# Six edits to a hand-ordered Trainium2 kernel: the order's port model, small GpSimd instructions, the sample tile last, and the first two weight loads

## The chip, the cores and the metric

The kernel runs on one NeuronCore of one Trainium2 chip. The metric is the device time of one execution in microseconds (us), the median of several runs. The engines are TensorE (PE in the profile, its weight loads PEld), VectorE (DVE), ScalarE (ACT), GpSimd (POOL) and SyncE (SP), which issues all DMAs of the kernel before.

## What is computed

One inference step of a one-layer encoder with three groups of heads, for a prompt of 512 tokens (four tiles of 128) and a sample of 32 tokens that has caches. Cut to what matters:

```
z = rmsnorm(x, g) @ w_in                   # 1024 -> 3880 columns, split below
A: qa, ka, va, ga   6 heads x 64           # chunk-band attention with a position bias
B: qb, kb, vb, gb   6 heads x 64, rotary   # attention to the best 128 (sample: 256) keys per query
   qi, ki, wi       8 x 32, 32, 8          # the indexer that scores the keys for B
M: qm, gm           4 heads x 64           # attention to 256 memory tokens, keys mk, mv from w_mem_kv
x = x + concat(oA*silu(ga), oB*silu(gb), oM*silu(gm)) @ w_out
y = rmsnorm(x, g_final)
```

Outputs are y for prompt and sample, and the new keys and values. All is float32. Where a product has to be exact enough, an operand is split into a part rounded to the fast float32r form (names that end in h) and the rest (names that end in l), and three products are added: h·h, l·h and h·l.

## The kernel before

**The order is made at build time.** `Line` (line 47) keeps a clock for each engine and a time at which each region of a tile will be ready. Every instruction is issued through `Timed` (253), which advances these clocks by a cost (`cost`, 67). Work is written as generators that yield the time at which they want to go on; a heap runs the earliest. So the position of an instruction in its engine's queue follows from modelled times, while on the chip each queue runs in order and waits on semaphores for what it needs. `port` (166) models that VectorE and GpSimd can't both use the SBUF port that they share: an instruction that would start while the other engine holds the port is moved to the end of that stretch. `least` and `scaled` choose between engines by these clocks. `warm` (727) puts matmuls of an identity matrix into TensorE's queue where the model sees a wait before the first real group is done.

**The head.** `x_load` (630) loads the transposed x in four pieces of two 128-row blocks, the first piece in two DMAs; three buffers, so the fourth waits for the first piece to be used up. `w_load` (473) loads weight pieces in the order of `w_list`; the first four are the indexer's (2 blocks x 296 columns = 592). `START` (36) is the order of the loads on SP's queue: w a weight piece, x a piece of x, t the rotary tables, r natural rows for the norms, m memory rows. `x_split` (651) makes xTh on ScalarE (an activation with scale g) and xTl on VectorE, block by block; `w_split` (488) makes wh on ScalarE and wl on VectorE for pieces 0 and 2 (`WV`), on GpSimd for all others. `index_group` (816) is the first real work of TensorE: four chunks (c = 0 to 3), each with a weight piece and two blocks of x, each for the token tiles 1, 2, 3, 0 with three products per block. It needs xTh, xTl, wh and wl of its chunk. After it come the sample's rows (`w_sample`) and the projections of `EARLY` and `LATE` (43, 44), attention, and the output projection.

**Norms and small instructions.** `norms` (686): ScalarE squares and sums a tile, GpSimd adds EPS, raises to -0.5 (rs) and divides by 16 (r16). `i_done` (799) copies and scales the indexer's head weights wI with rs, then r16, on GpSimd. `load_tables` (763) scales the rotary tables by rs on GpSimd, in eight instructions of 128x64. The load of the memory gain gT[1] is issued after all of `START` (751).

**The tail.** `out_part` (1639) makes the output projection. The last loop (1716) goes over two halves of 512 columns, and in each over the tiles in the order NT, 0, 1, 2, 3, where NT is the sample (32 rows, computed as 64 rows of two halves). A prompt tile takes 18 matmuls of 256 columns, the sample tile 12. For the last tile (`apart`) the 512 columns are evicted in two pieces of 256. `residual` (1670) adds x on VectorE, for the sample in two instructions; `settle` (1689) sums squares on ScalarE, adds up the pieces' sums (VectorE for all but the last piece, with a pointer operand), adds and takes the power on GpSimd, scales one half of the row on VectorE and the other on ScalarE (on VectorE for tile NT - 2), and stores the row.

## Time and profile before

| | us |
|---|---|
| median of 3 runs | 363.46 (363.11 to 363.86) |
| the profiled execution, its own time | 362.68 |
| its span, first to last instruction | 360.6 |
| TensorE busy within the span | 350.7 (97%) |
| VectorE / ScalarE / GpSimd busy | 276.6 / 219.6 / 191.0 |
| granted TensorE clock, mean | 0.996 |

The span is what the trace shows; the profiled execution took 2.1 us more than its span. Times in the trace count from the span's start. Matmul ends are modelled, so a matmul's duration is longer than the step to the next one; where steps matter, starts are compared. A row of the timeline gives start, duration, engine, line, operation, output and inputs, form and count, and in brackets the idle time of the engine before it and what ended that. Nearly all instructions carry the line of `Timed` (L273), so groups are told apart by tiles.

### The profile page before, as it was taken

How to read it: one execution, taken by the hardware profiler on the slowest of the kernel's cores; microseconds unless marked ns; L12 is line 12 of the kernel's file. 1: busy time of each engine (PE TensorE's matmuls, PEld its weight loads, DVE VectorE, ACT ScalarE, POOL GpSimd, SP SyncE). 2: the span in 40 equal slices, each digit the busy share in tenths (PEclk: the TensorE clock that was granted, in tenths of full speed). 3: DMA queues.
4: the chain of work that ended last, by engine and by line, in shares of the span. 5: the costliest groups of instructions: out<-in, count | busy, mean ns of one | idle time of the engine just before them, and what ended most of it. 6: DMA issues, size and time to landing. Idle time of an engine off the chain costs nothing.

```text
span 360.6 us, 7941 instructions
## 1 busy us (share of the span) xinstructions
PE 350.7 (97%) x2961; PEld 320.0 (89%) x2961; DVE 276.6 (77%) x696; ACT 219.6 (61%) x521; POOL 191.0 (53%) x213
## 2 busy tenths in 40 slices
PE   8999999999999999999999999999999999999991
PEld 8989988999998989898699898999979878888991
DVE  3665977797888978888999885999868576866463
ACT  5856767896747775595856553217665665544443
POOL 1778983375465574148436464534597412140751
PEclk9999999999999999999999999999999999999998
DMA  7998351475493322531203250133489412000015
GB/s 251 362 362 264 97 176 58 126 202 147 119 293 119 88 52 62 182 90 44 90 3 87 88 166 20 51 108 115 128 294 362 133 45 104 2 2 2 0 40 209
DMA packets 41478, 46.35 MB, mean 129 GB/s; under 512 B 5184, under 2 KB 36544, under 8 KB 41440
## 3 DMA queue, kind: packets, MB, share of 16 engines
q1 hardware_dynamic: 41440, 45.85, 39.9%
q8 instruction: 23, 0.38, 0.4%
q14 instruction: 15, 0.12, 0.1%
HBM read 39.67 MB, written 6.16 MB: 127 GB/s over the span
## 4 chain that ended last, share of the span: by engine, by line
PE 89%; DVE 4%; DMA 2%; issue 1%; ACT 1%; POOL 1%; SPq 1%; POOLq 0%; ACTq 0%; DVEq 0%
PE bank L273 89%; DMA raw<-in_w_in_dram 2%; POOL ss L273 1%; DVE ysel L273 1%; ACT sq L273 1%; DVE xr L273 1%; SPq L273 1%; DVE z L273 1%; DVE m L273 0%; DVE xTl L273 0%; DVE gate L273 0%; ACT wh L273 0%; ACT xTh L273 0%; DVE o L273 0%; DVE pt L273 0%
## 5 line engine op out<-in xcount | busy, mean ns | idle before, releaser
L273 POOL TENSOR_TENSOR wl<-raw,wh 128x512 fp32r<-128x512 f32 (+2 forms) x68 | 110.0, 1622 | 78.2 <-ACT wh L273 74.4
L273 ACT ACTIVATE wh<-raw 128x512 fp32r<-128x512 f32 (+2 forms) x70 | 50.1, 719 | 33.1 <-issue 13.6
L273 PE MATMUL bank<-wh,xTh 128*128 128x384 f32 (+1 forms) x192 | 65.3, 340 | 0.0
L273 PE MATMUL bank<-wl,xTh 128*128 128x384 f32 (+1 forms) x192 | 63.3, 330 | 0.0
L273 PE MATMUL bank<-wh,xTl 128*128 128x384 f32 (+1 forms) x192 | 63.2, 329 | 0.1
L273 ACT ACTIVATE z<-z,st 128x256 f32<-128x256 f32 (+3 forms) x77 | 41.0, 550 | 21.0 <-DVE st L273 20.9
L273 PE MATMUL bank<-xTh,wh 128*128 128x272 f32 x208 | 46.3, 304 | 0.0
L273 PE MATMUL bank<-xTh,wl 128*128 128x272 f32 x208 | 43.0, 288 | 0.0
L273 PE MATMUL bank<-xTl,wh 128*128 128x272 f32 x208 | 43.0, 288 | 0.0
L273 PEld LDWEIGHTS bank<-wh,xTh 128*128 128x128 f32 x192 | 36.1, 188 | 2.3 <-issue 1.6
L273 PEld LDWEIGHTS bank<-wh,xTl 128*128 128x128 f32 x192 | 36.2, 189 | 0.4 <-DVE xTl L273 0.3
L273 PEld LDWEIGHTS bank<-wl,xTh 128*128 128x128 f32 x192 | 36.1, 188 | 0.2 <-POOL wl L273 0.2
L273 PEld LDWEIGHTS bank<-xTh,wh 128*128 128x128 f32 x208 | 32.7, 189 | 1.7 <-issue 0.8
L273 PEld LDWEIGHTS bank<-xTh,wl 128*128 128x128 f32 x208 | 32.6, 189 | 0.1
L273 PEld LDWEIGHTS bank<-xTl,wh 128*128 128x128 f32 x208 | 32.6, 188 | 0.0
L273 DVE MAX8 m<-ysel 128x8 f32<-128x256 f32 (+2 forms) x48 | 26.4, 549 | 0.0
L273 DVE MATCH_REPLACE8 ysel<-m,ysel 128x256 f32<-128x256 f32 (+2 forms) x48 | 26.1, 543 | 0.0
L273 PE MATMUL bank<-ident,z 128*128 128x128 f32 (+1 forms) x161 | 25.0, 273 | 0.0
L273 ACT COPY pt<-bank 128x512 f32<-128x512 f32 (+1 forms) x26 | 14.1, 543 | 14.3 <-PE bank L273 14.2
L273 DVE SCALAR_TENSOR_TENSOR ysel<-r,wI,ysel 128x256 f32<-128x256 f32 (+2 forms) x21 | 17.8, 849 | 6.0 <-ACT r L273 5.6
L273 POOL TENSOR_TENSOR oBl<-o,oBh 128x128 fp32r<-128x128 f32 (+1 forms) x9 | 4.9, 549 | 30.4 <-ACT oBh L273 30.4
L273 PEld LDWEIGHTS bank<-ident,z 128*128 128x128 f32 (+1 forms) x161 | 18.2, 140 | 2.5 <-issue 1.0
(307 smaller groups left out, 892.6 us busy)
## 6 DMA issues: line engine op xcount, KB each, us to landing
raw<-in_w_in_dram SPq DMA_DIRECT2D x20, 384.0 KB, 3.6
raw<-in_w_in_dram SPq DMA_DIRECT2D x26, 256.0 KB, 2.9
raw<-in_w_out_dram SPq DMA_DIRECT2D x8, 384.0 KB, 3.1
nat<-in_x_prompt_dram SPq DMA_DIRECT2D x4, 512.0 KB, 7.9
raw<-in_w_mem_kv_dram SPq DMA_DIRECT2D x8, 256.0 KB, 2.8
xr<-in_x_prompt_dram SPq DMA_DIRECT2D x4, 512.0 KB, 4.8
out_dram<-xr SPq DMA_DIRECT2D x4, 512.0 KB, 2.6
xr<-in_x_t_dram SPq DMA_DIRECT2D x3, 544.0 KB, 5.8
```

The source lines that it names most:

```text
L273: return fn(*args, **kw)
```

## The change

Six things are changed.

- **Port model.** In `port`, a VectorE instruction is pushed behind GpSimd's stretch once and then stops; a GpSimd instruction is pushed only in a narrower case for VectorE (`kept`), and a VectorE instruction that takes the port pushes GpSimd's clock by its own length. GpSimd's memsets and one-column instructions get costs of their own.
- **First loads.** gT[0] and the weight pieces 0 and 1 are issued on ScalarE's queue, ahead of all else; SP's queue begins with x. `START` loses the two w's and is put in another order.
- **Weight piece 0.** Both wh and wl are made on VectorE, block by block, and chunk 0 of `index_group` runs block by block: all four tiles with xTh·wh, then xTh·wl, then xTl·wh.
- **Small instructions.** EPS is added on VectorE; r16 goes, the 1/16 sits in ScalarE's copy of wI, and wI is scaled by rs twice in one GpSimd instruction. The rotary tables' scaling waits until two units of attention are scored. In `settle`, the running sum of a later piece goes from VectorE to GpSimd.
- **gT[1]** is loaded with the first tables.
- **The tail.** The sample tile comes last in both halves and is the one that is evicted in two pieces; the row half on VectorE is that of tile 3, not 2.

```diff
-START = "wxwxwxwtwwwwrrrrrmmrr"
+START = "xxwwxtwwwwrrrrrmmrr"
...
+        if op == "memset":
+            return 0.05 + n / 1000.0
+        if n == 1:
+            return 0.57 if kw.get("op") == ALU.pow else 0.22
         return 0.15 + n * (0.0034 if op == "tensor_scalar" else 0.0021)
...
         for s, end, by in self.taken:
-            if by != eng and s <= t < end:
+            if by != eng and s <= t < end and (eng == "POOL" or t > self.kept + 0.02):
                 t = end
+                if eng == "DVE":
+                    break
+        if eng == "DVE":
+            if self.clk["POOL"] > t:
+                self.clk["POOL"] += d
+            self.kept = t + d
...
+    DMA2 = Timed(line, "ACTQ", nc.scalar)
...
-            DMA.dma_start(raw, w[k * P:(k + nk) * P, lo:hi].rearrange("(k p) n -> p k n", p=P))
+            (DMA2 if i < 2 else DMA).dma_start(raw, w[k * P:(k + nk) * P, lo:hi].rearrange("(k p) n -> p k n", p=P))
...
+            if i == 0:
+
+                wh = pw.tile(list(raw.shape), F32R, tag="wh", name="wh", bufs=n)
+                wl = pw.tile(list(raw.shape), F32R, tag="wl", name="wl", bufs=n)
+                for k in range(2):
+                    yield line.at(raw) - 0.2
+                    V.tensor_copy(wh[:, k], raw[:, k])
+                    tsub(V, wl[:, k], raw[:, k], f(wh)[:, k])
+                split.append((wh, wl))
+                continue
...
-            G.tensor_scalar(ss[:n, i:i + 1], ss[:n, i:i + 1], EPS, None, op0=ALU.add)
+            V.tensor_scalar(ss[:n, i:i + 1], ss[:n, i:i + 1], EPS, None, op0=ALU.add)
             G.tensor_tensor(rs[:n, i:i + 1], ss[:n, i:i + 1], nhalf[:n], op=ALU.pow)
-            G.tensor_scalar(r16[:n, i:i + 1], rs[:n, i:i + 1], 1.0 / 16, None, op0=ALU.mult)
...
-    DMA.dma_start(gT[0], a["norm_mix_g"])
+    DMA2.dma_start(gT[0], a["norm_mix_g"])
     line.until(lambda g=x_load(): next(g, 1) == 1)
+    allowed[0] = 2
+    line.spawn(w_load())
+    line.until(lambda: len(raws) == 2)
...
         def scale():
+            yield from line.wait(lambda: count["scored"] > 1)
...
-            A.copy(wI[:, t, :], acc[:, 288:296])
+            A.activation(wI[:, t, :], acc[:, 288:296], AF.Copy, scale=1.0 / 16)
...
-            for r in (rs, r16):
-                G.tensor_scalar(wI[:, t, :], wI[:, t, :], r[:, t:t + 1], None, op0=ALU.mult)
+            r = rs[:, t:t + 1]
+            G.tensor_scalar(wI[:, t, :], wI[:, t, :], r, r, op0=ALU.mult, op1=ALU.mult)
...
+            for kk in range(2) if c == 0 else ():
+                for xs, ws in ((xTh, w[0]), (xTh, w[1]), (xTl, w[0])):
+                    for t in (1, 2, 3, 0):
+                        c0, c1 = (256, 288) if t == 0 else (0, 296)
+                        x = xs[0][:, kk, t * P:(t + 1) * P]
+                        yield x, ws[:, kk, c0:c1]
+                        PE.matmul(acc[t][:, c0:c1], x, ws[:, kk, c0:c1], start=(kk == 0 and xs is xTh and ws is w[0]), stop=False)
...
-            V.tensor_scalar(run, new, EPS if j == 0 else old, None, op0=ALU.add)
+            if j == 0:
+                V.tensor_scalar(run, new, EPS, None, op0=ALU.add)
+            else:
+                G.tensor_tensor(run, new, old, op=ALU.add)
...
-        if t == NT - 2:
+        if t == NT - 1:
...
-                          (NT, 0, 1, 2, 3), (NT - 1,) if c0 else ()))
+                          (0, 1, 2, 3, NT), (NT,) if c0 else ()))
```

## Rows read from the trace of the kernel before

**Rows 1.** The page: its first line, and busy time, share of the span and instructions of each engine.

```profile
span 360.6 us, 7941 instructions
PE 350.7 (97%) x2961; PEld 320.0 (89%) x2961; DVE 276.6 (77%) x696; ACT 219.6 (61%) x521; POOL 191.0 (53%) x213
```

**Rows 2.** Busy time by stretch (us from the span's start): length, then busy time and instructions of PE, PEld, DVE, ACT and POOL, granted clock, DMA share, GB/s. Two answers are put together here; the first two rows hold nothing but fillers on PE.

```profile
1.36:4.00 2.64, 2.64 (x12) 2.64 (x13) 0.00 (x0) 1.03 (x3) 0.28 (x2) 1.00 0.64 186
...
6.00:7.18 1.18, 1.18 (x12) 1.18 (x12) 0.99 (x2) 0.54 (x1) 0.00 (x0) 1.00 0.98 329
...
7.18:20.48 13.30, 13.25 (x101) 12.81 (x99) 8.98 (x11) 8.89 (x13) 9.31 (x8) 1.00 1.07 370
20.48:352.70 332.22, 331.47 (x2832) 301.36 (x2831) 263.02 (x678) 205.05 (x498) 178.57 (x192) 1.00 0.37 115
352.70:360.60 7.90, 0.15 (x2) 0.00 (x0) 2.46 (x6) 2.01 (x7) 1.49 (x4) 0.81 0.49 199
150.00:200.00 50.00, 49.62 (x435) 43.72 (x432) 45.72 (x130) 35.22 (x91) 26.95 (x25) 1.00 0.19 57
```

**Rows 3.** Who PE's weight load waited for over the whole span: us in total, times, longest.

```profile
PEld bank L273 <- DVE st L273: 1.3, 3, 0.7
...
PEld bank L273 <- ACT mTh L273: 0.4, 1, 0.4
```

**Rows 4.** The timeline of the first microseconds, PE: the fillers, and the first matmul of chunks 0, 1, 2 and 3 of the index group, with the one in chunk 1 that waited.

```profile
1.36 6.06 PE L273 MATMUL bank<-ident 128*128 128x128 f32 x32 [1.36 <-POOL nhalf L273]
7.18 0.38 PE L273 MATMUL bank<-wh,xTh 128*128 128x296 f32 x1
...
10.54 0.39 PE L273 MATMUL bank<-wh,xTh 128*128 128x296 f32 x1
...
11.58 0.40 PE L273 MATMUL bank<-wh,xTl 128*128 128x296 f32 x1
...
14.17 0.38 PE L273 MATMUL bank<-wh,xTh 128*128 128x296 f32 x1
...
17.28 0.38 PE L273 MATMUL bank<-wh,xTh 128*128 128x296 f32 x1
```

**Rows 5.** The timeline of SP's queue from 0: the first issues.

```profile
0.73 0.39 SPq L273 DMA_DIRECT2D g_mix<-in_norm_mix_g_dram  x1
1.18 0.89 SPq L273 DMA_DIRECT2D xr<-in_x_t_dram  x2
```

**Rows 6.** The timeline of ACT from 0; the wait for a DMA in brackets tells when it landed.

```profile
0.73 1.28 ACT L273 ACT_TABLE_LOAD   x1 [0.73 <-PEq L1768]
...
5.84 0.70 ACT L273 ACTIVATE wh<-raw 128x592 fp32r<-128x592 f32 x1 [0.28 <-DMA raw<-in_w_in_dram]
7.72 0.75 ACT L273 ACTIVATE xTh<-xr,g_mix 128x544 fp32r<-128x544 f32 x1 [1.19 <-DMA xr<-in_x_t_dram]
8.69 0.70 ACT L273 ACTIVATE wh<-raw 128x592 fp32r<-128x592 f32 x1 [0.21 <-DMA raw<-in_w_in_dram]
...
20.40 1.06 ACT L273 ACTIVATE junk<-nat 128x1024 bf16<-128x1024 f32 x1 [2.32 <-DMA nat<-in_x_prompt_dram]
```

**Rows 7.** The timeline of DVE from 0: the rest of weight piece 0, and the rests of two blocks of x (the fourth and the fifth).

```profile
6.57 0.78 DVE L273 TENSOR_TENSOR wl<-raw,wh 128x592 fp32r<-128x592 f32 x1 [0.19 <-ACT wh L273]
...
10.06 2.20 DVE L273 SCALAR_TENSOR_TENSOR xTl<-xr,g_mix,xTh 128x544 fp32r<-128x544 f32 x2 [0.76 <-ACT xTh L273]
```

**Rows 8.** Groups of DVE instructions by form over the whole span (count, busy us, mean ns of one): the copies from SBUF to SBUF.

```profile
L273 DVE CAST identR<-ident 128x128 fp32r<-128x128 f32 x1 | 1.3, 1328 | 0.0
L273 DVE COPY z<-ysS 64x1056 f32<-64x1056 f32 x1 | 1.1, 1129 | 0.0
```

**Rows 9.** The same for POOL: the gates' first instruction, and one of the small instructions of the norms.

```profile
L273 POOL TENSOR_TENSOR tg<-tg,gate 128x272 f32<-128x272 f32 x13 | 11.1, 857 | 3.5 <-ACT tg L273 3.5
...
L273 POOL TENSOR_SCALAR r<-rs 128x1 f32<-128x1 f32 x6 | 1.4, 233 | 0.5
```

**Rows 10.** Who ACT waited for, from 20 to 36 us.

```profile
ACT mTh L273 <- DMA g_mem<-in_norm_mem_g_dram: 3.4, 1, 3.4
```

**Rows 11.** The timeline of the last microseconds, DVE.

```profile
344.73 1.40 DVE L273 TENSOR_TENSOR xrS<-bank,xrS 32x512 f32<-32x512 f32 x2 [0.67 <-PE bank L273]
...
350.85 0.69 DVE L273 TENSOR_TENSOR xr<-bank,xr 128x512 f32<-128x512 f32 x1 [0.69 <-PE bank L273]
...
352.89 0.42 DVE L273 TENSOR_TENSOR xr<-bank,xr 128x256 f32<-128x256 f32 x1 [0.17 <-PE bank L273]
...
354.57 0.48 DVE L273 TENSOR_SCALAR xr<-xr,ss 128x512 f32<-128x512 f32 x1
354.97 0.21 DVE L273 TENSOR_SCALAR ss<-ss 128x1 f32<-128x1 f32 x1
356.17 0.75 DVE L273 SCALAR_TENSOR_TENSOR xr<-xr,ss,gf 128x512 f32<-128x512 f32 x1 [1.00 <-POOL ss L273]
```

**Rows 12.** The same stretch, ACT and POOL: the last sum of squares, and the last power.

```profile
353.54 0.42 ACT L273 ACTIVATE sq<-xr 128x256 f32<-128x256 f32 x1
...
355.59 0.55 POOL L273 TENSOR_TENSOR ss<-ss,nhalf 128x1 f32<-128x1 f32 x1
```

**Rows 13.** DMA issues of the whole span: count, KB each, median us from issue to landing: the stores of a prompt tile and of the sample tile.

```profile
out_dram<-xr SPq DMA_DIRECT2D x4, 512.0 KB, 2.6
...
out_dram<-xrS SPq DMA_DIRECT2D x1, 128.0 KB, 2.0
```

More of the change, by code (lines that the diff above doesn't have):

```diff
@@ L52, in __init__ @@
     def __init__(self):
-        self.clk = dict.fromkeys(("PE", "DVE", "ACT", "POOL", "SP", "DMA"), 0.0)
+        self.clk = dict.fromkeys(("PE", "DVE", "ACT", "POOL", "SP", "ACTQ", "DMA"), 0.0)
         self.ready, self.used = {}, {}
@@ L58, in __init__ @@
         self.mode = None
-        self.taken = []
+        self.taken, self.kept = [], -1.0
         self.tasks = []
@@ L177, in op @@
             t = max(t, self.had(x, eng))
-        if eng == "SP":
+        if eng in ("SP", "ACTQ"):
             self.clk[eng] = t + 0.05
@@ L182, in op @@
             self.clk["DMA"] = end
+            eng = "SP"
         else:
@@ L385, in hybrid_step @@
     m8 = cp.tile([P, 8], F32, name="m8")
-    rs, r16, ss = (cp.tile([P, 8], F32, name=n) for n in ("rs", "r16", "ss"))
+    rs, ss = (cp.tile([P, 8], F32, name=n) for n in ("rs", "ss"))
     normed = set()
@@ L733, in hybrid_step @@
     line.warm = warm
-    line.spawn(w_load())
     for g in (w_split(), w_sample(), x_split(), norms(), m_split(), spread()):
@@ L750, in start @@
                 load_tables(32)
-        DMA.dma_start(gT[1], a["norm_mem_g"])
+                DMA.dma_start(gT[1], a["norm_mem_g"])
         allowed[0] = len(w_list)
@@ L820, in index_group @@
             line.until(lambda: x_done[0] > c)
+            for kk in range(2) if c == 0 else ():
[5 more added lines that the diff above has]
+                        PE.matmul(acc[t][:, c0:c1], x, ws[:, kk, c0:c1], start=(kk == 0 and xs is xTh and ws is w[0]), stop=False)
             for t in (1, 2, 3, 0):
-                yield needs_of(xTh, xTl, w, c, t)
-                tokens(acc[t], xTh, xTl, w, c, t, *((256, 288) if t == 0 else (0, 296)), c == 0, c == NK // 2 - 1)
+                if c > 0:
+                    yield needs_of(xTh, xTl, w, c, t)
+                    tokens(acc[t], xTh, xTl, w, c, t, *((256, 288) if t == 0 else (0, 296)), False, c == NK // 2 - 1)
                 if c == NK // 2 - 1:
```

## The prediction

> **What bounds the kernel now.** First read the page's busy line [rows 1]: TensorE is busy for 97% of the span. A share says little by itself, so next cut the span where TensorE's work begins and ends [rows 2]. From 20.48 to 352.70 us it is busy for 331.47 of 332.22 us: there is no hole for another engine to fill or to empty, and with the same matmuls in the same number this stretch can give little. Outside it lie three stretches that the change touches: 7.18 us ahead of the first real matmul, with fillers alone; the index group from 7.18 to 20.48 us; and 7.90 us behind the last matmul, of which VectorE works 2.46 and ScalarE 2.01 us. Last come the waits of the weight load [rows 3], because a matmul's modelled end hides short waits: no engine costs it more than 1.3 us in the whole span. So I look for the gain at both ends, and expect from the middle only what another order of the same work does.
>
> The profiled execution took 362.68 us, 2.08 more than its span, and 0.78 less than the median of 363.46. I make the sum against the former and add 0.78 at the end.
>
> **The head: what sets it.** Chunk 1 of the index group begins at 10.54 us, and a matmul in it waits to 11.58 [rows 4]. Chunk 2, which waits for nothing, takes 17.28 - 14.17 = 3.11 us; chunk 1 took 14.17 - 10.54 = 3.63, so 0.52 went into waits. The matmul at 11.58 waited for the rest of x's fourth block: VectorE's row at 10.06 holds two of these, 2.20 us, and the second ends at 12.26 [rows 7]. It was late because ScalarE had xTh of block 3 at 7.72, when the second piece of x landed, then waited for weight piece 1 (8.69) and rounded that for 0.70 us before it could go to block 4 [rows 6]. So the index group's end hangs on the second piece of x and on weight piece 1, not on the moment at which TensorE starts.
>
> **The head: the sum.** The gain load leaves SP's queue: x is issued at 0.73 instead of 1.18 us [rows 5], 0.45 earlier. On ScalarE's queue three issues of some 0.43 us each (half of the two at 1.18 [rows 5] is 0.45) stand ahead of the table load, which then runs from about 2.1 to 3.4 and ends before the first block of x can land. That x piece 0, weights 0 and 1 and x piece 1 have landed was at 8.69 before; the same bytes 0.45 us earlier are there at 8.2, x piece 1 last. From there count ScalarE 2 x 0.75 for two blocks (row at 7.72), and VectorE 0.2 behind each, 0.78 each, one behind the other: the fourth block's rest is ready 0.05 + 0.75 + 0.1 + 2 x 0.8 = 2.5 us after the landing, at 10.7. Before, TensorE had 14.17 - 11.58 = 2.59 us of chunk 1 left at that point; so chunk 1 ends at about 13.35 instead of 14.17, a gain of 0.82. Bounds: if x piece 1 lands at 7.72 as before, 1.3; if at 8.69, 0.35. I take 0.82, because the 16 DMA engines are full from 7.18 to 20.48 us (370 GB/s) and already at 0.98 in the microsecond before [rows 2]: a second queue can put loads in another order, but their sum takes as long.
>
> Splitting weight piece 0 on VectorE in halves: the rest of 592 columns takes 0.78 [rows 7], half about 0.45. No row has a half copy; the nearest are 1129 ns for 1056 columns, by length 0.32 for 296, and 1328 ns for a 128-column cast that fell together with GpSimd's work [rows 8]. I take 0.4, next to the first, since GpSimd has only a short gain product in this time. Then TensorE starts at about 5.4 (landing of the weights, 5.84 less 0.45 [rows 6]) + 0.4 + 0.1 = 5.9 us, at worst 6.9. Chunk 0 takes 3.1 us and has to be done by 13.35 - 3.11 = 10.25, so any start up to 7.15 gives the same end: of the 1.3 us that TensorE starts earlier, 0.5 turn into a longer wait in chunk 1. The two copies and rests stand ahead of the second block's rest in VectorE's queue, 1.7 us; that too is inside the slack.
>
> The share of 0.98 to 1.07 in these stretches [rows 2] comes from one queue alone; what two do to each other no row shows. The Trainium skill, DMA: Bandwidth & Descriptors, section "Issuing engines are not separate DMA queues", speaks against this part of the change: transfers that several engines issue run on the same 16 DMA engines and interleave, and only the time to issue them is saved. By that rule the landing at 8.2 holds and the total is the 361.5 below; if the queues didn't hinder each other, x piece 1 would land at 7.72 or before and the total would be 361.0.
>
> **The tail.** Now a prompt tile of 18 matmuls ends the kernel. The last residual starts at 352.89 [rows 11], the last sum of squares at 353.54 [rows 12] and it is read by about 354.05. Then VectorE is in the way: it scales tile 2's row (to 355.05) before the one-column sum at 354.97, which ends 355.18 [rows 11]; GpSimd adds and takes the power from 355.59 to 356.14 [rows 12]; the row is scaled at 356.17 and stored with 512 KB, 2.6 us from issue to landing, where the sample's 128 KB took 2.0 [rows 13]. With the sample last, its second piece leaves TensorE at the same moment; its two residuals of 256 columns take 2 x 0.42 instead of 0.42, + 0.42. Tile 3 ends 12 matmuls earlier, 12/18 of the 2.04 us between the residuals at 350.85 and 352.89, 1.36 us. In the bad case tile 2's scaling (0.75) and the sample's first residuals stand between, the sample's sum is read at 355.25, the row is scaled at 356.15, as before, and only the smaller store counts: 0.65. In the good case there is no such block, and since the one-column sum is on GpSimd (0.2 and 0.55 us), the scaling starts at 355.7: 0.47 + 0.6 = 1.1. Tile 3's store is then issued at about 355.7 and lands at 358.3, ahead of the sample's. I take 0.9.
>
> **The rest.** gT[1]: ScalarE waited 3.4 us for it [rows 10], and TensorE 0.4 us for mTh [rows 3]. The load moves ahead of six weights and seven row loads on SP's queue, which costs these 0.4 us of issue while DMA is full anyway; I take 0.2 of the 0.4. Small GpSimd instructions: seven r16 and three wI products fall away, 0.23 each [rows 9]; GpSimd is busy for 53% [rows 1] and nothing on TensorE's path waits for it, so nothing. Seven EPS sums move to VectorE, about 0.2 each, covered as long as VectorE isn't held by them (below). Port model: no instruction of its own; another order in the middle, where I take 0 and bounds of 1 us either way, about what all engines' waits there could give.
>
> Sum: 362.68 - 0.82 - 0.9 - 0.2 = 360.76; with 0.78, **361.5 us**.
>
> **The rivals.** *The head gives nothing* (chance 0.19): x piece 1 lands no earlier because both queues share the engines, or VectorE stands behind an EPS sum. ScalarE's first square waited 2.32 us for its rows [rows 6]; a sum that waits for it in VectorE's queue holds the evictions of the index group behind it, and with them PSUM banks. For it speaks that DMA is full, against it that four more banks are free. Then only the tail counts: 363.46 - 0.9 - 0.2 = 362.4. *The middle gains too* (0.12): the new port model keeps VectorE and GpSimd apart, and the 1328 ns cast [rows 8] is such a collision. One us of waits less gives 360.2. *VectorE becomes the bound* (0.07): the model pushes GpSimd's clock, so the order gives VectorE work that GpSimd had, such as the gates' 13 pairs of 0.86 us [rows 9]. From 150 to 200 us VectorE is busy for 45.72 of 50 [rows 2]; from 4.3 us more in it TensorE waits for each further one; with 7.3, 3 us: 364.5. *The clock rises late* (0.05): twelve fillers take 2.64 us ahead of 4 us and 1.18 us after 6 [rows 2], though both rows say 1.00: the pace doubled, from the 1.2 to the 2.4 GHz level, after some 4.7 us of gapless fillers. If the earlier start brings gaps before that, and the pace stays at the lower level through chunks 0 and 1, each takes 3.1 us more; from 13.35 the end moves to 5.9 + 12.4 = 18.3: 361.5 + 4.9 = 366.4, slower. It decides once the rise comes later than about 9 us. That leaves 0.57 for the forecast.
>
> **How the numbers follow.** About 0.2% (0.73 us) can be told from no change, so faster is below 362.73 and slower above 364.19. The forecast with its bounds is 360.6 to 362.4, nearly all faster; the first rival at 362.4 lies two thirds on that side; the third and fourth are slower. That gives 0.74 faster, 0.15 within, 0.11 slower. The range takes in the better middle from 360.0 and, above, the first rival with its bounds and part of the fourth, 364.0.
>
> **What would show it.** Right: x issued at 0.73; chunk 1 ends near 13.35 and chunk 3 near 19.6; the last matmul to the span's end takes 7.0 instead of 7.9; no one-column sum on VectorE among the last rows; ScalarE's wait for the memory gain gone. Wrong: chunk 2 starts at 14 or later (first rival); waits of the weight load for VectorE of several us between 100 and 250 (third); matmul steps twice as long after 7 us (fourth); or a span between the index group and the last matmul that differs from 332.2 by over 1 us, since then the order of the middle has done more than both ends.

## The result and the profile after

| | before | after |
|---|---|---|
| median, us | 363.48 (363.11 to 363.86, 4 runs) | 365.54 (364.65 to 365.75, 4 runs) |
| profiled execution, us | 362.68 | 364.65 |
| its span | 360.6 | 362.9 |

The ratio is 1.0058 [1.0046, 1.0071]: the change costs 2.1 us, where 361.5 us was forecast. The page's first line and its busy line, against [rows 1]:

```profile
span 362.9 us, 7961 instructions
PE 351.6 (97%) x2971; PEld 320.8 (88%) x2971; DVE 281.5 (78%) x711; ACT 215.8 (59%) x517; POOL 180.4 (50%) x191
```

No share tells where 2.3 us of span went. The stretches do; they are cut at the first real matmul, at the sample's first matmul behind the index group, and behind the last matmul, as in [rows 2]:

```profile
6.16:21.11 14.95, 14.62 (x114) 14.24 (x112) 12.01 (x16) 9.21 (x14) 11.10 (x8) 1.00 1.03 349
21.11:355.46 334.35, 331.99 (x2832) 301.76 (x2831) 264.42 (x688) 201.03 (x493) 165.16 (x169) 1.00 0.37 114
355.46:362.90 7.44, 0.16 (x2) 0.00 (x0) 3.64 (x7) 2.54 (x8) 2.29 (x5) 0.76 0.55 209
```

The index group ends at 21.11 us (20.48 before: + 0.63). The same 2832 matmuls behind it take 334.35 us (332.22: + 2.13). What follows the last matmul takes 7.44 us (7.90: - 0.46). The sum is + 2.30. In the middle TensorE's idle time rose from 0.75 to 2.36 us, its busy time from 331.47 to 331.99.

**The head.** PE's timeline in the index group, beside [rows 4], and then ACT, DVE and POOL, beside [rows 6, 7]:

```profile
6.16 0.67 PE L285 MATMUL bank<-wh,xTh 128*128 128x296 f32 x4
...
9.79 0.40 PE L285 MATMUL bank<-wh,xTh 128*128 128x296 f32 x1 [0.33 <-ACT xTh L285]
10.03 1.72 PE L285 MATMUL bank<-ident 128*128 128x128 f32 x14
11.51 0.38 PE L285 MATMUL bank<-wh,xTl 128*128 128x296 f32 x1
...
12.00 0.39 PE L285 MATMUL bank<-wh,xTl 128*128 128x296 f32 x1
...
14.59 0.38 PE L285 MATMUL bank<-wh,xTh 128*128 128x296 f32 x1
...
21.11 1.20 PE L285 MATMUL bank<-raw,xF 128*32 128x296 f32 x16
```

```profile
1.17 0.98 ACTq L285 DMA_DIRECT2D raw<-in_w_in_dram  x2
...
8.40 0.70 ACT L285 ACTIVATE wh<-raw 128x592 fp32r<-128x592 f32 x1 [2.93 <-DMA raw<-in_w_in_dram]
9.00 2.01 ACT L285 ACTIVATE xTh<-xr,g_mix 128x544 fp32r<-128x544 f32 x3
```

```profile
5.42 0.40 DVE L285 CAST wh<-raw 128x296 fp32r<-128x296 f32 x1
...
9.77 1.42 DVE L285 SCALAR_TENSOR_TENSOR xTl<-xr,g_mix,xTh 128x544 fp32r<-128x544 f32 x1 [2.03 <-ACT xTh L285]
```

```profile
9.18 1.44 POOL L285 TENSOR_TENSOR wl<-raw,wh 128x592 fp32r<-128x592 f32 x1 [3.52 <-ACT wh L285]
```

TensorE starts 1.0 us earlier, but chunk 1 takes 4.80 us (9.79 to 14.59), so chunk 2 starts 0.42 us later than before. ScalarE waited 2.93 us for weight piece 1 with the blocks of x queued behind it. GpSimd then made that weight's rest beside VectorE's rest of x's third block, which took 1.42 us; the second block's, at 6.97 with nothing beside it, took 0.78. So the rest of the fourth block was ready only at 11.93 us, and its matmul started at 12.00. Behind the first matmul of chunk 1 stand 14 fillers, which end before that.

**The middle.** Behind the head, two waits of the weight load are over 0.7 us here; the longest of before was 0.7 [rows 3]:

```profile
PEld bank L285 <- ACT pt L285: 1.4, 1, 1.4
...
PEld bank L285 <- ACT vb L285: 1.0, 1, 1.0
```

The first of them, PE and then ACT: TensorE's transposes at 245.92 wait for a bank that ScalarE empties at 245.30, behind two weight roundings.

```profile
245.92 0.66 PE L285 MATMUL bank<-ident,z 128*128 128x128 f32 x4 [1.14 <-ACT pt L285]
```

```profile
243.74 0.83 ACT L285 ACTIVATE wh<-raw 128x768 fp32r<-128x768 f32 x1
...
244.78 0.61 ACT L285 ACTIVATE wh<-raw 128x512 fp32r<-128x512 f32 x1
245.30 0.56 ACT L285 COPY pt<-bank 128x512 f32<-128x512 f32 x1
```

Such waits are the idle time. Busy time can hide a loss too, where the same matmuls take longer. Groups of PE by form (busy us, mean ns of one) of the last pass, before and then after:

```profile
L273 PE MATMUL bank<-wh,oBh 128*128 128x256 f32 x48 | 13.2, 276 | 0.0
L273 PE MATMUL bank<-wl,oBh 128*128 128x256 f32 x48 | 13.2, 276 | 0.0
```

```profile
L285 PE MATMUL bank<-wh,oBh 128*128 128x256 f32 x48 | 13.5, 281 | 0.0
L285 PE MATMUL bank<-wl,oBh 128*128 128x256 f32 x48 | 13.5, 281 | 0.0
```

5 ns more per matmul with nothing waiting: from start to start 117 to 118 ns instead of 113 to 114. Over all 543 matmuls that move 256 weight columns, steps of 160 ns and more left out, the mean step is 117.8 ns instead of 115.3: 1.3 us.

**The tail.** DVE, beside [rows 11]: the sample's last residuals (second pair, 356.51) stand behind a row scaling.

```profile
355.75 0.73 DVE L285 SCALAR_TENSOR_TENSOR xr<-xr,ss,gf 128x512 f32<-128x512 f32 x1
356.51 0.86 DVE L285 TENSOR_TENSOR xrS<-bank,xrS 32x256 f32<-32x256 f32 x2
```

### The profile page after: what moved, and what is told of

The parts are those of the page before. It is cut to its first block, busy times and chain, and to the rows that moved or that the text cites. A ratio compares the mean times of both kernels' runs of the same rounds, so it can differ in the third digit from the quotient of the medians.

```text
span 362.9 us, 7961 instructions
## 1 busy us (share of the span) xinstructions
PE 351.6 (97%) x2971; PEld 320.8 (88%) x2971; DVE 281.5 (78%) x711; ACT 215.8 (59%) x517; POOL 180.4 (50%) x191
## 3 DMA queue, kind: packets, MB, share of 16 engines
HBM read 39.67 MB, written 6.16 MB: 126 GB/s over the span
## 4 chain that ended last, share of the span: by engine, by line
PE 84%; DVE 10%; DMA 2%; ACT 1%; POOL 1%; issue 1%; ACTq 0%; POOLq 0%; DVEq 0%
PE bank L285 84%; DMA raw<-in_w_in_dram 2%; DVE rank L285 1%; DVE ysel L285 1%; DVE rt L285 1%; DVE qb L285 1%; DVE st L285 1%; DVE m L285 1%; DVE xrS L285 1%; DVE mTl L285 1%; DVE bf_t L285 1%; DVE kst L285 0%; DVE vbS L285 0%; POOL wl L285 0%; DVE qbS L285 0%
## 5 line engine op out<-in xcount | busy, mean ns | idle before, releaser
L285 POOL TENSOR_TENSOR wl<-raw,wh 128x512 fp32r<-128x512 f32 (+2 forms) x68 | 108.6, 1603 | 91.9 <-ACT wh L285 89.7
L285 PE MATMUL bank<-wh,xTh 128*128 128x384 f32 (+1 forms) x192 | 64.3, 340 | 0.3 <-ACT xTh L285 0.3
L285 PE MATMUL bank<-wl,xTh 128*128 128x384 f32 (+1 forms) x192 | 62.2, 329 | 0.0
L285 ACT ACTIVATE z<-z,st 128x256 f32<-128x256 f32 (+3 forms) x76 | 40.1, 544 | 37.1 <-DVE st L285 37.1
L285 ACT COPY pt<-bank 128x512 f32<-128x512 f32 (+1 forms) x28 | 15.0, 539 | 20.3 <-PE bank L285 20.3
L285 PEld LDWEIGHTS bank<-ident,z 128*128 128x128 f32 (+1 forms) x161 | 18.2, 140 | 4.7 <-ACT pt L285 1.4
L285 DVE TENSOR_TENSOR xr<-bank,xr 128x256 f32<-128x256 f32 (+1 forms) x24 | 12.1, 509 | 12.5 <-PE bank L285 12.4
L285 DVE SCALAR_TENSOR_TENSOR ysel<-r,wI,ysel 128x256 f32<-128x256 f32 (+2 forms) x21 | 16.9, 805 | 5.5 <-ACT r L285 4.8
```

The source lines that it names most:

```text
L285: return fn(*args, **kw)
```

## The experiments

Names that begin with a_ are the changed kernel with an edit, those with b_ the kernel before with one. All times are medians; a ratio is to the kernel before, run on the same chip.

### Addresses: a_pad, b_pad32, b_pad64, a_nohead

r16 was 32 bytes in each partition of SBUF. With it gone, every later tile on that side moved down by 32 bytes, weight pieces and oBh, oBl among them; oAh, oMh and oS stayed. The edits put bytes back (a_pad) or add some.

```diff
 # a_pad
-    rs, ss = (cp.tile([P, 8], F32, name=n) for n in ("rs", "ss"))
+    rs, pad, ss = (cp.tile([P, 8], F32, name=n) for n in ("rs", "pad", "ss"))
 # b_pad32; b_pad64 has 16 columns for pad
-    rs, r16, ss = (cp.tile([P, 8], F32, name=n) for n in ("rs", "r16", "ss"))
+    rs, r16, pad, ss = (cp.tile([P, 8], F32, name=n) for n in ("rs", "r16", "pad", "ss"))
```

a_pad. 

> The changed kernel with one unused tile of 32 bytes per partition in the place where r16 was, so that every SBUF tile lies at the same address as in the kernel before; no instruction and no place in a queue differs from the changed kernel. Theory A (taking r16 away moved the weight pieces by 32 bytes, to multiples of 64, and matmuls of 256 columns that read them step 117 to 118 ns instead of 113 to 114): the step in the last pass is 113 to 114 ns again and the time falls by about 1.8 us, to 363.7. Theory B (the slower step comes from the order or from the chip's state, not from addresses): the step stays at 117 and the time at 365.5.

Measured 364.3 us, 1.0016 [1.0003, 1.0028]; theory A rather than B, though the time fell by 1.2 and not by 1.8. The mean step is 115.5 ns, and the stretch from the group's end to the last matmul takes 332.96 us, 1.39 less than in the changed kernel. The last pass, against the 281 ns above:

```profile
L285 PE MATMUL bank<-wh,oBh 128*128 128x256 f32 x48 | 13.2, 276 | 0.0
L285 PE MATMUL bank<-wl,oBh 128*128 128x256 f32 x48 | 13.2, 276 | 0.0
```

b_pad32. 

> The kernel before with one unused tile of 32 bytes per partition added behind r16, which moves the weight pieces from 32 to 0 past a multiple of 64 (192 past a multiple of 256); no instruction differs. Theory A, in its form for 64 bytes: the 256-column step is 117 ns and the time rises by 1.0 to 1.9 us, to 364.5 to 365.4. Theory A in a form for 128 bytes (a multiple of 64 that is not one of 128 is harmless), or theory B: step 113, time 363.5.

Measured 364.15 us, 1.0017 [1.0009, 1.0026], between the times of the two theories; the pass over oAh and oAl is slower, the last is not. The first line is the kernel before, the others b_pad32:

```profile
L273 PE MATMUL bank<-wl,oAh 128*128 128x256 f32 x48 | 13.3, 278 | 0.0
L273 PE MATMUL bank<-wl,oAh 128*128 128x256 f32 x48 | 13.5, 281 | 0.0
L273 PE MATMUL bank<-wl,oBh 128*128 128x256 f32 x48 | 13.3, 276 | 0.0
```

b_pad64. 

> The kernel before with 64 unused bytes behind r16 in place of 32: the weight pieces then lie at 224 past a multiple of 256, 32 past a multiple of 64 as in the kernel before, and at the same place as the attention outputs that they meet. Theory A1 (it counts whether both operands lie at the same place past a multiple of 64): 256-column step 113 to 114 ns in both passes, time 363.4. Theory A2 (it counts that they lie 64 apart past a multiple of 128): step 115 to 118 and 364.2, as with 32 bytes.

Measured 363.99 us, 1.0021 [1.0005, 1.0037]: A2 rather than A1. The table has the steps of 256-column matmuls with 128 columns of stationary operand: the place (address past a multiple of 128 bytes) of the moving weights and of the next matmul's stationary operand, the median step in ns, and the share of steps of 116 ns and more. The trace has no addresses; the places follow from the sizes and the order of the tiles.

```
               weights, oA  median  share    weights, oB  median  share
before           32, 96      114     31%       32, 96      113      0%
a_pad            32, 96      117     52%       32, 96      113      1%
a_nohead_pad     32, 96      114     40%       32, 96      114     49%
b_pad32          64, 96      117     93%       64, 0       113      0%
b_pad64          96, 96      120     99%       96, 32      113      1%
changed kernel    0, 96      117     83%        0, 64      118    100%
a_nohead          0, 96      117     82%        0, 64      113      1%
```

Theory A holds in its general form: the same instructions in the same order take 1.2 us more or less by medians when SBUF tiles move by 32 bytes, and b_pad32 and b_pad64 lose 0.8 and 0.7 us on the kernel before. But the place isn't the whole rule. Where the two lie 64 bytes apart, both levels of the step occur; elsewhere over 80% of the steps are slow. At one and the same place the last pass is slow in the changed kernel and fast in a_nohead, and in a_nohead_pad its first half steps 118 ns and its second 113. That profile is the slowest of eleven runs (365.26), so the level may differ between executions of one kernel; with one or two profiles of each it isn't shown how often. The medians over 12 runs of a_pad and 10 of the changed kernel don't hang on that.

a_nohead undoes the diff's edits to START, DMA2, the split of weight piece 0 and chunk 0. 

> The changed kernel with its loads, the split of weight piece 0 and chunk 0 as before (the edits to START, DMA2, the split on VectorE and the block-by-block chunk undone); port model, small instructions, gT[1] and tail stay changed, and so does the 32-byte shift. Theory H (the new head costs what the traces show, 0.6 us): the index group ends at 20.5 us instead of 21.1 and the time is 364.9. Rival (the head's loss is taken up by the order of the middle): 365.5. In either case the 256-column step stays at 117 ns if it hangs on the addresses.

Measured 364.67 us, 1.0038 [1.0026, 1.0050]. The index group ended at 21.02 us, by 0.1 less than in the changed kernel, so theory H fell, though the time is lower by 0.9. The step did not stay at 117 ns in the last pass, where it is 113.

### The parts: b_tail, b_head, b_port, a_noport_pad, b_slack

b_tail has the edits to settle and to the last loop alone. 

> The kernel before with the tail's edits alone: the sample last and evicted in two pieces, the row half on VectorE for tile 3, the running sum on GpSimd; addresses as before. Theory T (the tail keeps what it gave between the last matmul and the end, 0.47 us, wherever it stands): 363.0. Rival (nothing, since the sample's residuals wait behind tile 3's scaling on VectorE): 363.4. By the prediction: 362.6.

Measured 363.13 us, 0.9991 [0.9982, 1.0000]: a gain of 0.25 us, between theory T and its rival, and less than the 0.9 of the prediction.

after_again is the changed kernel once more. 

> The changed kernel once more, unaltered, beside the parts below and profiled a second time. Two things of the first profile are in question. First, the index group ended at 21.1 us where the one profile of the kernel before has 20.48, but three kernels with the old head ended it at 21.0 to 21.3: theory H1 (20.48 was an early landing; the ends of both heads differ by less than 0.2 us) expects 20.9 to 21.3 here; theory H2 (the new head is late by 0.6) can't be told by this run alone. Second, the last 144 matmuls of prompt tiles stepped 117 ns with operands at 0 past a multiple of 64, while in the run without the new head the same addresses gave 113: if that was the state of one execution, the step here can be 113. Time 365.5 (2.1 us above the kernel before).

Measured 365.53 us, 1.0061 [1.0037, 1.0086]; the group ends at 21.58 us, and the last pass steps 117 to 118 ns again, in all of its matmuls.

a_nohead_pad is a_nohead with the 32 bytes of a_pad. 

> The changed kernel with the old head and with 32 unused bytes where r16 was, so that all addresses are those of the kernel before; left of the change are port model, small instructions, gT[1] and tail. If the parts add up: the shift costs 1.1 us (changed kernel less the one with the unused tile) and the head 0.8 (changed kernel less the one without the new head), so this gives 365.5 - 1.9 = 363.6, against 363.4 for the kernel before. Theory O (each edit reorders the middle anew, and what an edit costs hangs on that order, so parts don't add up): any time from 362.5 to 364.5, and the difference stands between 60 and 335 us of the trace, not at the ends.

Measured 364.17 us, 1.0020 [1.0009, 1.0030], against a_pad's 364.3: with the addresses of before the new head, together with the order that it draws, is worth nothing either way. Of the 0.9 us between the changed kernel and a_nohead, 0.5 stand in the last pass, whose first to last matmul on oBh and oBl took 17.7 us in a_nohead and 18.2 in the changed kernel.

b_port has the edits to port and cost alone. 

> The kernel before with the port model and the costs of memsets and one-column instructions alone: no instruction is added or taken away, only the order in the queues (and the engine where the planner chooses one) differs; addresses as before. Theory O: a difference of up to 1 us either way, here expected slower, +0.4 (what is left of the changed kernel's 2.1 us after the shift, the head and the tail). Rival (the order is worth nothing): 363.4. The prediction's rival (the middle gains): 362.4.

Measured 371.92 us, 1.0217 [1.0190, 1.0245]. Its profiled run is its fastest, 369.42 us. A few single waits hold most of that run's loss, of PE in total, times, longest:

```profile
PE bank L284 <- ACT bf_ok L284: 1.8, 1, 1.8
PE bank L284 <- DVE z L284: 1.7, 1, 1.7
...
PE bank L284 <- DVE KSs L284: 1.3, 1, 1.3
```

b_head has the head's edits alone. 

> The kernel before with the new head alone: three loads on the ScalarE queue, weight piece 0 split on VectorE, chunk 0 block by block; addresses as before. Theory H1 (both heads end the index group at the same time): end of the index group at 20.9 to 21.3 us and 363.4, plus or minus what the new order of the middle gives. Theory H2 (the new head costs 0.6 to 0.8): 364.1. By the prediction: 19.6 us and 362.6.

Measured 365.43 us, 1.0050 [1.0033, 1.0067]; the group ends at 21.59 us, and the middle is longer by other waits than in the changed kernel.

a_noport_pad takes the port model out of the changed kernel. 

> The changed kernel without the port model and its costs, with 32 unused bytes where r16 was (addresses of the kernel before). The port model alone cost the kernel before 8.5 us, the whole change with these addresses costs 0.9. If the parts added up, the change without the port model would take 363.4 + 0.9 - 8.5 = 355.8 us. Theory O (each edit draws a new order of the middle, and the loss is a handful of single waits that this order happens to hold): nothing near that, 362.5 to 365, with the waits of the weight load between 7 and 12 us in the sum.

Measured 381.4 us, 1.0500 [1.0486, 1.0513], far above what was expected. The parts don't add up, and the bounds of theory O were too narrow.

b_slack. 

> The kernel before with one constant of the order's model changed by less than one per cent (SLACK 1.31 for 1.3): no instruction is meant to change, but the order of TensorE, VectorE and ScalarE differs from about 100 us on in many places. It measures what a new order by itself does. Theory O: a difference of 0.3 to 2 us, more likely slower (the kernel before has 6.8 us of waits of the weight load, the others so far 7.1 to 11.7): 364.4. Rival (the order matters only where the port model is wrong): 363.4 within 0.3.

```diff
-SLACK = 1.3
+SLACK = 1.31
```

Measured 379.4 us, 1.0445 [1.0418, 1.0472]: 16 us from one digit. PE, the wait that starts it, and two stretches (granted clock in the column before the last two):

```profile
270.50 0.48 PE L273 MATMUL bank<-k,ql 64*128 64x128 f32 x2 [4.77 <-DVE ql L273]
```

```profile
260.00:270.00 10.00, 5.27 (x51) 4.57 (x49) 8.43 (x14) 5.99 (x17) 6.10 (x6) 0.97 0.54 190
270.00:280.00 10.00, 9.38 (x69) 8.04 (x70) 9.21 (x27) 5.36 (x20) 4.39 (x5) 0.69 0.32 98
```

A wait of 4.77 us costs more than itself: behind it the granted clock is 0.69, so TensorE is back at the 1.2 GHz level for more than half of the next 10 us. The model chooses engines too: five instructions of b_slack went from VectorE to ScalarE net (691 and 526 on its page, 696 and 521 before), so order and choice aren't told apart. Every order that these runs drew anew was slower than that of the kernel before, by 0.7 to 18 us. So that order is a good one among those seen. The changed kernel's is one of the better ones, with the two waits shown above.

### The tail's port: b_tail4

The edit is to the kernel of b_tail.

```diff
+        if t in (NT - 2, NT - 1):
+            yield from line.wait(lambda: last)    # set behind the sample's last sum of squares
...
-        if t == NT - 1:
-            V.tensor_scalar(y[:rows, 0:512], y[:rows, 0:512], run, None, op0=ALU.mult)
-        else:
-            A.activation(y[:rows, 0:512], y[:rows, 0:512], AF.Copy, scale=run)
+        A.activation(y[:rows, 0:512], y[:rows, 0:512], AF.Copy, scale=run)
```

> The kernel before with the tail's edits and two more: the row scalings of tiles 2 and 3 are put behind the sample's last sum of squares in the queues of VectorE and ScalarE, and no tile has both row halves on VectorE. Nothing else in any queue differs from the run with the tail's edits. Theory T2 (the tail gave only 0.25 to 0.5 us because the sample's last residuals stood 0.8 us behind a row scaling on VectorE): the last sample residual starts within 0.4 us of the last matmul's start, the sample is stored at 357.3 instead of 358.0 and the time is 362.5. Rival (the stores of tiles 2 and 3, now later, end last): 363.0.

Measured 363.75 us, 1.0007 [0.9998, 1.0016]: theory T2 fell, and the rival's 363.0 too. POOL in b_tail, then DVE and POOL in b_tail4:

```profile
355.54 0.18 POOL L273 TENSOR_TENSOR ss<-ss 32x1 f32<-32x1 f32 x1
356.29 0.18 POOL L273 TENSOR_TENSOR ss<-ss 32x1 f32<-32x1 f32 x1 [0.57 <-ACT sq L273]
```

```profile
354.86 1.39 DVE L273 SCALAR_TENSOR_TENSOR xr<-xr,ss,gf 128x512 f32<-128x512 f32 x2
```

```profile
354.87 1.44 POOL L273 TENSOR_TENSOR ss<-ss 32x1 f32<-32x1 f32 x1
...
356.64 0.54 POOL L273 TENSOR_TENSOR ss<-ss,nhalf 32x1 f32<-32x1 f32 x1
```

The residuals came 0.6 us earlier (all four are done by 354.9), though the last still started 1.0 us behind the last matmul. But now both row scalings run beside the sample's one-column sums on GpSimd. The first of these took 1.44 us instead of 0.18 and ended at 356.30, where the second scaling ended at 356.25; the second sum waited for the first, and the sample was stored at 358.01, as in b_tail (358.00). The Trainium skill, SBUF — State Buffer, section "Who interferes with whom", says that a VectorE instruction with two SBUF inputs contends with a GpSimd instruction that reads SBUF, through the pair of ports that they share, and that this pair is an exclusive lock; these rows agree. The sample's store took 2.6 us from issue to landing instead of 1.9, which is why b_tail4 is slower than b_tail with a store issued at the same time. That the later store of tile 2 slows it is likely, but not shown.

### A place for x: b_tail_xpad

```diff
     xp = pool(xpx, "xp", "left")
+    xp.tile([P, 16], F32, name="pad")
```

> The kernel before with the tail's edits and 64 unused bytes ahead of the rounded x (xTh, xTl), which moves x from 32 to 96 past a multiple of 128 while the weight pieces stay at 32. No instruction differs from the run with the tail's edits (363.1). The 256-column matmuls stepped 113 to 114 ns where moving and next stationary operand lay 64 apart past a multiple of 128 and 115 to 119 otherwise; the 480 matmuls of 384 columns have met only equal places so far, and step 175. Theory A2, if it holds for every width: the 384-column step falls to 167 to 170 and the time by 2.4 to 3.8 us, to about 360. Theory A2 for 256 columns alone (the 272-column matmuls have met both places at 124 to 126): 175 as before, 363.1.

Measured 362.56 us, 0.9975 [0.9961, 0.9989], the fastest of all. The 384-column matmuls in b_tail, then here:

```profile
L273 PE MATMUL bank<-wh,xTh 128*128 128x384 f32 x160 | 56.1, 350 | 0.0
```

```profile
L273 PE MATMUL bank<-wh,xTh 128*128 128x384 f32 x160 | 55.6, 347 | 0.0
```

The median step fell from 175 to 173 ns in two of the three products, 320 matmuls, and stayed in the third: 0.6 us, a fifth of what A2 for every width promised.

### The head: a_headx, a_nofill, a_headx_nofill, a_nofill_xpad

All four have the 32 bytes of a_pad.

```diff
 # a_headx, in w_split, ahead of the wait for the landing
+            if i == 1:
+                yield from line.wait(lambda: line.had(xTh[0][:, 3, :]) > 0)
 # a_nofill, in index_group; a_headx_nofill has both, a_nofill_xpad this one and the place for x
             line.until(lambda: x_done[0] > c)
+            if c == 1:
+                line.warm = None
```

a_headx. 

> The changed kernel with the addresses of before (32 unused bytes) and one edit to the head: on the ScalarE queue the rounding of weight piece 1 stands behind the rounding of the two blocks of the second piece of x, not ahead of them. Theory Q (the new head gave nothing because ScalarE waited 2.9 us for weight piece 1, issued second on its queue and slowed by SP's loads, with blocks that had landed by about 6.5 us queued behind it): chunk 2 starts at 13.5 us instead of 14.6 to 15.1 and the index group ends at 20.0 to 20.4 instead of 21.1 to 21.6. Rival D (the landings set it, whatever the queue order): 14.6 and 21.1 or later. The rest of the order is drawn anew by the planner, so the whole time says little: anywhere from 363 to 380.

Measured: chunk 2 at 15.02, the group's end at 21.3, 369.06 us, 1.0165 [1.0129, 1.0200]. ACT, POOL and PE:

```profile
7.33 1.39 ACT L285 ACTIVATE xTh<-xr,g_mix 128x544 fp32r<-128x544 f32 x2 [1.89 <-DMA xr<-in_x_t_dram]
8.62 0.68 ACT L285 ACTIVATE wh<-raw 128x592 fp32r<-128x592 f32 x1
```

```profile
9.38 1.53 POOL L285 TENSOR_TENSOR wl<-raw,wh 128x592 fp32r<-128x592 f32 x1 [1.53 <-ACT wh L285]
```

```profile
10.53 0.30 PE L285 MATMUL bank<-wh,xTl 128*128 128x296 f32 x1
10.67 1.73 PE L285 MATMUL bank<-ident 128*128 128x128 f32 x14
12.15 0.38 PE L285 MATMUL bank<-wl,xTh 128*128 128x296 f32 x1
```

The second piece of x had landed at 7.3. With it ahead, VectorE began both rests of chunk 1 before GpSimd began the weight's, and they took 0.78 us each, the second to 9.59. The rest of weight piece 1 was there at 10.91; its matmul started at 12.15, behind 14 fillers, which cost 1.2 us here. Theory Q's numbers didn't come, but it isn't refuted: the fillers took its gain.

a_nofill. 

> The changed kernel with the addresses of before (32 unused bytes), and no matmuls of the identity once chunk 1 of the index group has begun; the rest of every queue is that of the run with the 32 bytes alone. In that run, 14 such fillers stand between the first and the second real matmul of chunk 1, from 10.0 to 11.4 us, though the rest of x that the second one needs was ready at about 10.5 and the rest of the weights at 10.6. Theory F (the fillers hold up the real work, because the order's model has its operands later than the chip): chunk 2 starts at 14.0 to 14.2 instead of 14.55, the index group ends 0.4 to 0.5 us earlier, and the time falls from 364.3 to 363.8. Rival (the next rest of x, ready at about 11.3, sets it anyway): 14.5 and 364.3.

Measured 364.15 us, 1.0024 [1.0010, 1.0039], against a_pad's 364.3: no gain to speak of, as the rival had it. The expectation has the rest of x's third block ready at about 10.5; in a_pad's trace it takes VectorE 1.45 us beside GpSimd and is ready at 11.16. The fourth block's follows at 11.89, and its matmul starts at 11.95, when the fillers are over. From there to chunk 2 it is 2.6 us in a_pad (14.55), in the changed kernel (14.59) and in the kernel before (11.58 to 14.17).

Where the loads land late, the missing fillers cost time. The profiled run (365.41, its runs go from 362.88 to 365.43) is such a one; PE, and stretches:

```profile
11.76 0.41 PE L285 MATMUL bank<-wh,xTl 128*128 128x296 f32 x1 [1.08 <-DVE xTl L285]
```

```profile
12.00:14.00 2.00, 2.00 (x9) 1.70 (x9) 2.00 (x4) 2.00 (x5) 1.20 (x2) 0.56 0.98 271
14.00:16.00 2.00, 2.00 (x12) 2.00 (x10) 2.00 (x2) 1.97 (x3) 2.00 (x3) 0.59 0.97 340
```

TensorE had nothing to do but one matmul from 10.28 to 11.76, and its granted clock was 0.56 and 0.59 in the stretches from 12 to 16 us; its 296-column steps took about 246 ns instead of 135, chunk 2 started at 16.49, and the group ended at 22.81. In after_again weight piece 1 came as late (8.87, here 8.88), but with the fillers the clock stayed at 1.00 and the group ended at 21.58. So in this order the fillers hold up nothing, and they hold the clock. The other runs agree: the five above 364.7 us have a mean granted clock of 0.989 to 0.992, the seven below of 0.994 to 0.997.

a_headx_nofill. 

> As the run with weight piece 1 rounded behind the second piece of x, and without the 14 fillers in chunk 1 (and two ahead of it). There the rest of weight piece 1 was ready at 10.9 us, but the matmul that needs it started at 12.15, behind the fillers. Theory Q with F (the head's gain was lost to ScalarE's queue order and to the fillers): chunk 2 starts at 13.6 to 13.9 and the index group ends at 20.0 to 20.2, which is the prediction's 13.35 and 19.6 within 0.5. Rival D (landings): 14.5 and 21.0 or later. The order behind the head is a new one, so the whole time says little.

```profile
11.17 0.40 PE L285 MATMUL bank<-wl,xTh 128*128 128x296 f32 x1 [0.15 <-POOL wl L285]
...
14.05 0.38 PE L285 MATMUL bank<-wh,xTh 128*128 128x296 f32 x1
...
20.37 0.46 PE L285 MATMUL bank<-raw,xF 128*32 128x296 f32 x4
```

Chunk 2 at 14.05 and the group's end at 20.37, 0.7 to 1.2 us before the three ends of the changed order (21.07, 21.11, 21.58), nearer to theory Q with F than to D. The operands came early enough that no long gap was left. But six profiles of the old head end between 20.07 and 21.47, so this one profile doesn't show a gain over it. Its whole time, 373.9 us, 1.0290 [1.0270, 1.0310], is that of a bad order behind it.

a_nofill_xpad. 

> The changed kernel mended at three places: addresses of before (32 unused bytes), no fillers in chunk 1, and 64 unused bytes ahead of x as in the fastest run so far. The parts add up here, since no order is drawn anew: 364.3, less 0.5 for the fillers, less 0.6 for the place of x: 363.2, the time of the kernel before within 0.3. Rival (the place of x gives nothing in this order): 363.8.

Measured 364.1 us, 1.0020 [1.0006, 1.0035]: the 0.5 us of the fillers didn't come, as in a_nofill, and the 0.6 of the place of x doesn't show in the median either, although the 384-column step is 173 ns again in the same two products. In its profiled run, 362.36, weight piece 1 came at 7.94 and the clock stayed at 1.00; chunk 2 started at 14.14, again 2.6 us behind the matmul of the fourth block's rest (11.56). The six slowest of its twelve runs have a mean granted clock of 0.990 to 0.992, the others of 0.995 to 0.997, so here too both cases occur.

## Why the prediction was wrong

- **"Small GpSimd instructions: ... so nothing".** The largest single error. As engine time it was right; but the tile r16 went with its instructions, and moving the operands of TensorE by 32 bytes cost 1.2 us by medians (365.5 against 364.3 in a_pad). I read what the instructions do and not where the tiles lie, and no rival had it.
- **The head, 0.82.** It gave nothing. The last of the four loads was there at 8.40, for 8.2 in the sum, but the step "x piece 1 last" failed: x's second piece landed first (7.3) and weight piece 1 last, and the ScalarE queue had that weight ahead of x. So its rounding, 0.60 us, came before the blocks, and GpSimd's rest of it ran beside VectorE's rest of the third block, which took 1.42 us where the sum has 0.78 for each. The rows held this price: the 2.20 us of [rows 7] are 1.47 beside GpSimd and 0.81. The fourth block's rest, forecast for 10.7, was ready at 11.93, and chunk 2 began at 14.59 instead of 13.35; the 2.6 us between them were right. In this order the fillers cost nothing; with weight piece 1 behind x (a_headx) they do, and with both undone chunk 2 started at 14.05. And the profile of before was an early one: six profiles with the head of before end the group at 20.07, 20.48, 21.15, 21.28, 21.44 and 21.47 us, so the + 0.63 of the table is within what landings do by themselves. The first rival, "the head gives nothing", had this part right but put it down to x landing no earlier; it landed earlier and wasn't used. Its sign, chunk 2 at 14 or later, came true.
- **The Trainium skill's rule on issuing engines** (DMA: Bandwidth & Descriptors, section "Issuing engines are not separate DMA queues") agrees with the trace: with two queues the gain load took 3.2 us from issue to landing, where SP alone took 1.6, and weight piece 1 was only 0.3 us earlier (8.40 for 8.69) although it was issued at about 1.66.
- **Splitting weight piece 0 on VectorE** was sized well: copies of 0.40 and 0.30 us for the 0.4 taken, TensorE's start at 6.16 for 5.9. The EPS sums on VectorE held nothing in the head: the first runs at 24.29 us.
- **The tail, 0.9.** Right in sign, off in size: 0.46 us in the trace, 0.25 [0 to 0.65] measured alone. It was the bad case, in which the sample's residuals stand behind a row scaling, and less than the 0.65 put down for that. The queue order of b_tail4 didn't bring the good case, since the scalings then hold up GpSimd's sums.
- **gT[1], 0.2.** Neither ScalarE's wait for the gain nor TensorE's for mTh [rows 3, 10] is in the trace after. Too small to be told in the sum.
- **The port model, "0 and bounds of 1 us either way".** The value nearly stood for this order: with the addresses of before, the middle is 0.7 us longer (332.96 in a_pad, 332.22 before), and the two waits shown are in a_pad as well. But the bounds were far too narrow: the port model alone (b_port) cost 8.5 us, and other edits that draw a new order up to 18. The waits of the old order (1.3 us at most for one engine) bound what a better order can gain, not what a worse one can cost. Nothing in the prediction told the fair order of the whole change from the bad one of b_port, so the value near 0 is luck.
- **VectorE as the bound, the clock's late rise.** Neither happened. The clock came into play from the other side, where a new order or the missing fillers left TensorE idle.
- The sign named last, a middle that differs from 332.2 by over 1 us, came true as well (334.35).

Sum by the runs: addresses + 1.2; all the rest together + 0.9 (a_pad). In that rest the tail gives back 0.25 to 0.46 us, so head and middle cost 1.2 to 1.4; the profiles show 0.7 of it in the middle, and what an execution's landings add to that isn't told apart. Left open: why the last pass of the changed kernel steps 117 to 118 ns at a place that is fast in a_nohead.

## What to carry to other kernels

Where an edit adds or removes a tile, look at where the operands of the matmuls behind it land, and put the bytes back before judging the edit. A tuned static order is one draw among many: an edit that its planner sees is timed together with a new order, so compare edits in kernels whose queues are otherwise equal, and bound the order by a planner change that means nothing. Price an instruction with what will run beside it: a merged row hides that one of two took nearly twice as long. One profile of a head that waits for DMAs is one sample; take several before calling 0.6 us a loss or a gain.

## What the runs showed of the hardware

- A float32r matmul of 256 columns stepped at one of two levels, 113 to 114 ns or 117 to 120, and moving tiles by 32 or 64 bytes changed which, with every instruction the same. Where the moving operand and the next stationary one lay 64 bytes apart past a multiple of 128, both levels occurred (0 to 100% slow steps, by run and tile); elsewhere over 80% of the steps were slow. For 384 columns it is 173 against 175 in two of three products. The Trainium skill, SBUF — State Buffer, section "Who interferes with whom", gives TensorE two independent read ports, for the moving operand and for the weights, and names no such effect; the measurement decides. The reason isn't known.
- In a_nofill's head TensorE waited 0.34 and 1.08 us with one matmul between, and 4 us at a granted clock of 0.56 to 0.59 followed; in b_slack a wait of 4.77 us was followed by 10 us at 0.69. Fillers of 1.7 us, which look like waste, cost nothing in the changed order and kept the clock.
- A one-column sum on GpSimd took 1.44 us instead of 0.18 beside two two-input VectorE instructions of 0.7 us. In the head it was the other way round: VectorE's rest of a block of x, with two inputs, took 1.42 us beside GpSimd's rest of a weight piece, and 0.78 without.
